# Row sums of 16384 x 1024 floats on one core: a two-row column tail, a first load of 4 rows, and the second group's load held until those are summed

## Chip, core, metric

One core of one Trainium2 chip. The metric is the device time of one execution in microseconds (us). The profile's span (first to last instruction) is 1.7 to 1.8 us shorter than the time of the same execution.

## The reference

```python
batch, seq, dim = 32, 512, 1024
x = np.random.randn(batch, seq, dim).astype(np.float32)     # 67.1 MB
def reference(x):
    return np.sum(x, axis=-1).astype(np.float32)            # 16384 sums
```

One addition for every four bytes read: the work is reading x once.

## The kernel before

Every partition gets 128 rows, in eight groups of 16. A group is one load of 8.39 MB (64 KB for each partition) into one of three buffers. VectorE sums the groups; in the last two groups ScalarE takes part of the rows, and the last row comes in three column pieces so that little is left to sum after the last byte.

```python
    nbig = J // BIG - 1                 # 7 groups of BIG = 16 rows, then a tail
    tail = [(8, 4), (4, 2), (2, 1)]     # rows, and how many of them ScalarE sums
    ...
        def act(dst, src, n):
            nc.scalar.activation(out=scratch[:, :n], in_=src,
                                 func=mybir.ActivationFunctionType.Copy, accum_out=dst)
    ...
        for i in range(nbig):
            t = inpool.tile([P, BIG * dim + 2], fp32)
            rows_of(t, 0, BIG, i * BIG, BIG // 2 if i == nbig - 1 else 0)
            if i % 3 == 2:
                store(nc.gpsimd, i - 2, i + 1)
        store(nc.gpsimd, nbig - 1, nbig)
    ...                                 # 8, 4, 2 rows, then one row for ScalarE
        cuts = [0, 384, 768, dim]       # the last row, in three column pieces
        for c0, c1 in zip(cuts, cuts[1:]):
            nc.sync.dma_start(out=last[:, c0:c1], in_=rows_from(j, 1)[:, 0, c0:c1])
        for i, (c0, c1) in enumerate(zip(cuts, cuts[1:])):
            if c1 < dim:
                vec(last[:, dim + i : dim + i + 1], last[:, c0:c1])
            else:                       # the third piece with the two partial sums
                vec(sums[:, j : j + 1], last[:, c0 : dim + i])
        store(nc.sync, nbig, nbig + 1)
```

(`...` marks what is left out.) The first load is moved ahead of the start-up barrier, to the very beginning of the program; loads 2 and 3 are issued right after the barrier.

## Time and profile before

| | before |
|---|---|
| time, median of 3 (range) | 162.79 us (162.73 to 162.85) |
| the profiled execution: time, span | 163.31 us, 161.5 us |
| hardware DMA queue, share of 16 engines' span | 97.1% |
| VectorE busy | 75% |
| 16-row sums start apart | 19.35 us, so 8.39 MB / 19.35 us = 433.5 GB/s |

The page of the profile of before. A queue's line gives packets, MB and the time of its packets as a share of sixteen DMA engines' span; a group's line gives busy time and mean ns, then the idle time before it and what ended it.

```profile
span 161.5 us, 124 instructions
...
DVE 121.4 (75%) x13; ACT 19.7 (12%) x33; POOL 2.4 (1%) x7
...
q1 hardware_dynamic: 2160, 67.12, 97.1%
q0 software_dynamic: 96, 0.06, 0.1%
...
L66 DVE TENSOR_REDUCE sums<-t 128x16 f32<-128x16384 f32 (+5 forms) x11 | 120.4, 10941 | 37.1 <-DMA t<-in_x_dram 37.0
```

Loads bound the kernel: their queue is busy nearly throughout, and all of VectorE's idle time ends with a load. The timeline of before, its start and its end (start and duration in us; the bracket is the idle time before and what ended it):

```profile
22.41 17.22 DVE L66 TENSOR_REDUCE sums<-t 128x16 f32<-128x16384 f32 x1 [22.41 <-DMA t<-in_x_dram]
41.74 17.22 DVE L66 TENSOR_REDUCE sums<-t 128x16 f32<-128x16384 f32 x1 [2.12 <-DMA t<-in_x_dram]
...
78.62 0.87 POOL L88 DMA_DIRECT2D out_dram<-sums  x1 [78.18 <-DVE sums L66]
...
138.55 8.69 DVE L66 TENSOR_REDUCE sums<-t 128x8 f32<-128x8192 f32 x1 [2.15 <-DMA t<-in_x_dram]
...
157.09 1.06 ACT L71 ACTIVATE scratch<-t 128x1024 f32<-128x1024 f32 x1
157.64 1.01 DVE L66 TENSOR_REDUCE t<-t 128x1 f32<-128x384 f32 x2 [0.68 <-DMA t<-in_x_dram]
158.06 0.19 ACT L71 ACTIVATION_READ_ACCUMULATOR scratch<-t 128x1 f32 x1
158.68 0.42 DVE L66 TENSOR_REDUCE sums<-t 128x1 f32<-128x258 f32 x1
159.17 0.35 SPq L88 DMA_DIRECT2D out_dram<-sums  x1
```

The first group can be summed at 22.41 us, and the stream alone needs 19.35 us for it. The last load packet ends at 157.90 us and its landing is signalled at 158.37; VectorE is then still on the piece before, so the last sum, 0.42 us, starts at 158.68, and a store follows. More quantities come from the trace's records of single DMA packets. A 64 KB packet takes 2.418 us in the steady stream; the sixteen first ones took 3.57 us on average, 1.15 us more. That is called the **start loss** below: the time that packets which start in the first 10 us take over the usual time of their size, per engine. The usual time is 2.418 us for 64 KB, 1.815 for 48 KB, 1.213 for 32 KB and 0.611 for 16 KB, the medians.

### The profile page before, as it was taken

Reading aid. Unit: us, or ns where it says so; the run is one execution under the profiler, and the core shown is the slowest. Engines: PE = TensorE matmul, PEld = TensorE weight load, DVE = VectorE, ACT = ScalarE, POOL = GpSimd, SP = SyncE. Lnnn points to the kernel's source line nnn. Section 1 sums busy time; section 2 is a strip of 40 time slices with the busy share of each in tenths; the row PEclk is TensorE's granted clock in tenths of the full one; section 3 lists DMA queues with packets and bytes.
Section 4 is the critical chain, followed back from the end, with each engine's and each line's share of the span. In section 5 each row is a group of like instructions: output and inputs, shape, how many; then the busy total and the mean of one; then the engine's idle time right before and its main releaser. Section 6 shows DMA issues by size and latency. Waiting matters only on the chain.

```text
span 161.5 us, 124 instructions
## 1 busy us (share of the span) xinstructions
DVE 121.4 (75%) x13; ACT 19.7 (12%) x33; POOL 2.4 (1%) x7
## 2 busy tenths in 40 slices
DVE  0000049998699968999499994999949997697883
ACT  3000000000000000000000000000000000698891
POOL 0000000000000000000200000000000001001000
DMA  8997998997997997996996996996997996999990
GB/s 260 519 438 341 519 406 373 519 438 341 519 454 325 519 471 308 519 487 292 519 493 293 519 487 292 519 487 292 519 454 325 519 487 292 391 491 389 410 392 14
DMA packets 2256, 67.18 MB, mean 416 GB/s; under 512 B 416, under 2 KB 848, under 8 KB 976
## 3 DMA queue, kind: packets, MB, share of 16 engines
q1 hardware_dynamic: 2160, 67.12, 97.1%
q0 software_dynamic: 96, 0.06, 0.1%
HBM read 67.11 MB, written 0.07 MB: 416 GB/s over the span
## 4 chain that ended last, share of the span: by engine, by line
DMA 74%; DVE 22%; SPq 1%; issue 0%; DVEq 0%
DMA t<-in_x_dram 74%; DVE sums L66 22%; SPq L81 1%; DVE t L66 1%; DVEq L66 0%
## 5 line engine op out<-in xcount | busy, mean ns | idle before, releaser
L66 DVE TENSOR_REDUCE sums<-t 128x16 f32<-128x16384 f32 (+5 forms) x11 | 120.4, 10941 | 37.1 <-DMA t<-in_x_dram 37.0
L71 ACT ACTIVATE scratch<-t 128x1024 f32<-128x1024 f32 x16 | 16.9, 1057 | 137.8 <-DMA t<-in_x_dram 137.3
L88 POOL DMA_DIRECT2D out_dram<-sums x3 | 2.2, 732 | 146.2 <-DVE sums L66 135.4
L71 ACT ACTIVATION_READ_ACCUMULATOR scratch<-t 128x1 f32 x16 | 3.0, 186 | 0.0
L66 DVE TENSOR_REDUCE t<-t 128x1 f32<-128x384 f32 x2 | 1.0, 549 | 0.7 <-DMA t<-in_x_dram 0.7
L71 ACT ACT_TABLE_LOAD x1 | 1.3, 1283 | 0.8 <-PEq L135 0.8
L135 POOL MEMSET const-float32-0.0<- 128x1 f32 x1 | 0.1, 98 | 0.2 <-issue 0.2
L135 POOL MEMSET const-bfloat16-1.0<- 128x1 bf16 x1 | 0.1, 101 | 0.0
L135 POOL MEMSET const-uint8-127<- 128x1 uint8 x1 | 0.1, 99 | 0.0
L135 POOL MEMSET const-float32-1.0<- 128x1 f32 x1 | 0.1, 98 | 0.0
## 6 DMA issues: line engine op xcount, KB each, us to landing
t<-in_x_dram SPq DMA_DIRECT2D x1, 4096.0 KB, 31.2
t<-in_x_dram SPq DMA_DIRECT2D x1, 2048.0 KB, 35.9
t<-in_x_dram SPq DMA_DIRECT2D x1, 1024.0 KB, 37.8
t<-in_x_dram SPq DMA_DIRECT2D x1, 512.0 KB, 38.6
t<-in_x_dram SPq DMA_DIRECT2D x2, 192.0 KB, 38.6
t<-in_x_dram SPq DMA_DIRECT2D x1, 128.0 KB, 38.4
t<-in_x_dram SPq DMA_DIRECT2D x7, 40.8
out_dram<-sums POOLq DMA_DIRECT2D x2, 24.0 KB, 7.9
```

The lines of the kernel that those rows point to most:

```text
L66: nc.vector.tensor_reduce(out=dst, in_=src, axis=mybir.AxisListType.X, op=mybir.AluOpType.add)
L71: nc.scalar.activation(out=scratch[:, :n], in_=src, func=mybir.ActivationFunctionType.Copy, accum_out=dst,)
L81: nc.sync.dma_start(out=block, in_=rows_from(j, n))
L88: eng.dma_start(out=out_v[:, g0:g1], in_=sums[:, g0 * BIG : g1 * BIG].rearrange("p (g j) -> p g j", j=BIG),)
L135: nc = _bacc.Bacc("TRN2", target_bir_lowering=False, num_devices=1)
```

## The change

Its intent: let the stream start without descriptors of later loads in its way (4 rows first, the second group held until VectorE has summed them); put all but the last 16 sums of each partition into one store that ScalarE issues near the end, in place of three GpSimd stores; share the two last rows between VectorE and ScalarE in three column pieces (640, 256, 128); and let ScalarE's unread results go to PSUM. The diff also adds `tc.manual_schedule()`. The core of the diff (comments added):

```diff
-        tc.tile_pool(name="scratch", bufs=1) as spool,
+        tc.tile_pool(name="unread", bufs=4, space=bass.MemoryType.PSUM) as upool,
+        tc.manual_schedule(),
...
-        for i in range(nbig):
-            t = inpool.tile([P, BIG * dim + 2], fp32)
-            rows_of(t, 0, BIG, i * BIG, BIG // 2 if i == nbig - 1 else 0)
-            if i % 3 == 2:
-                store(nc.gpsimd, i - 2, i + 1)
-        store(nc.gpsimd, nbig - 1, nbig)
+        for g in range(last):
+            t = inpool.tile([P, BIG * dim + 4], fp32)
+            if g == 0:
+                rows(t, 0, FIRST, 0, 0)                      # FIRST = 4
+                first = sums_of[-1]
+                rows(t, FIRST, BIG - FIRST, FIRST, 0)
+                continue
+            load = rows(t, 0, BIG, g * BIG, BIG // 2 if g == last - 1 else 0)
+            if g == 1:
+                tc.add_manual_dep(load.ins, first.ins.name, ...)
...
+        for width in pieces:                                 # 640, 256, 128
+            if len(parts) == k:
+                at += k                                      # room for partial sums
+            part = t[:, at : at + 2 * width].rearrange("p (n d) -> p n d", n=2)
+            nc.sync.dma_start(out=part, in_=rows_from(j, 2)[:, :, c : c + width])
...
+        w = t[:, at - 2 * width - k : at + k]
+        for i, part in enumerate(parts[:k]):
+            vec(w[:, i : i + 1], part[:, 0, :])
+            act(w[:, k + 2 * width + i : k + 2 * width + i + 1], part[:, 1, :], pieces[i])
+        store(nc.scalar, 0, last)
+        vec(sums[:, j : j + 2], w.rearrange("p (n d) -> p n d", n=2))
+        store(nc.sync, last, last + 1)
```

More of the change, by code (lines that the diff above doesn't have):

```diff
@@ L51, in rows_from @@
         return x_g[j // BIG, :, j % BIG : j % BIG + n, :]
-    nbig = J // BIG - 1
-    tail = [(8, 4), (4, 2), (2, 1)]
+    last = J // BIG - 1
+    FIRST = 4
+    pieces = (640, 256, 128)
     with (
         tc.tile_pool(name="in", bufs=3) as inpool,
-        tc.tile_pool(name="scratch", bufs=1) as spool,
+        tc.tile_pool(name="unread", bufs=4, space=bass.MemoryType.PSUM) as upool,
         tc.tile_pool(name="stage", bufs=1) as stpool,
+        tc.manual_schedule(),
     ):
         sums = stpool.tile([P, J], fp32)
-        scratch = spool.tile([P, dim], fp32)
         def vec(dst, src):
-            nc.vector.tensor_reduce(
+            return nc.vector.tensor_reduce(
                 out=dst, in_=src, axis=mybir.AxisListType.X, op=mybir.AluOpType.add
@@ L70, in act @@
         def act(dst, src, n):
+            unread = upool.tile([P, dim], fp32)
             nc.scalar.activation(
-                out=scratch[:, :n],
+                out=unread[:, :n],
                 in_=src,
@@ L76, in act, with rows @@
             )
-        def rows_of(t, a, n, j, n_act):
+        sums_of = []
+        def rows(t, a, n, j, n_act):
             nv = n - n_act
             block = t[:, a * dim : (a + n) * dim].rearrange("p (n d) -> p n d", d=dim)
-            nc.sync.dma_start(out=block, in_=rows_from(j, n))
-            if nv:
-                vec(sums[:, j : j + nv], block[:, :nv, :])
+            load = nc.sync.dma_start(out=block, in_=rows_from(j, n))
+            sums_of.append(vec(sums[:, j : j + nv], block[:, :nv, :]))
             for q in range(nv, n):
                 act(sums[:, j + q : j + q + 1], block[:, q, :], dim)
+            return load
         def store(eng, g0, g1):
@@ L91, in store @@
             )
-        for i in range(nbig):
-            t = inpool.tile([P, BIG * dim + 2], fp32)
-            rows_of(t, 0, BIG, i * BIG, BIG // 2 if i == nbig - 1 else 0)
-            if i % 3 == 2:
-                store(nc.gpsimd, i - 2, i + 1)
-        store(nc.gpsimd, nbig - 1, nbig)
-        t = inpool.tile([P, BIG * dim + 2], fp32)
+        for g in range(last):
[7 more added lines that the diff above has]
+            if g == 1:
+                tc.add_manual_dep(
+                    load.ins,
+                    first.ins.name,
+                    mybir.DependencyInfo(mybir.DependencyClass.Sync, mybir.DependencyReason.DATA),
+                    reason="no descriptors of later loads while the first ones start",
+                )
@@ L102 @@
+        t = inpool.tile([P, BIG * dim + 4], fp32)
         a = 0
-        for n, n_act in tail:
-            rows_of(t, a, n, nbig * BIG + a, n_act)
+        j = last * BIG
+        for n in (8, 4, 2):
+            rows(t, a, n, j + a, n // 2)
             a += n
-        rows_of(t, a, 1, nbig * BIG + a, 1)
-        a += 1
-        j = nbig * BIG + a
-        last = t[:, a * dim :]
-        cuts = [0, 384, 768, dim]
-        for c0, c1 in zip(cuts, cuts[1:]):
-            nc.sync.dma_start(out=last[:, c0:c1], in_=rows_from(j, 1)[:, 0, c0:c1])
@@ L115 @@
-        for i, (c0, c1) in enumerate(zip(cuts, cuts[1:])):
-            if c1 < dim:
-                vec(last[:, dim + i : dim + i + 1], last[:, c0:c1])
-            else:
-                vec(sums[:, j : j + 1], last[:, c0 : dim + i])
-        store(nc.sync, nbig, nbig + 1)
+        j += a
+        at = a * dim
+        k = len(pieces) - 1
+        parts = []
+        c = 0
+        for width in pieces:
[3 more added lines that the diff above has]
+            nc.sync.dma_start(out=part, in_=rows_from(j, 2)[:, :, c : c + width])
+            parts.append(part)
+            at += 2 * width
+            c += width
```

## The prediction

> **What bounds the kernel now.** The DMA stream. The page shows hardware-queue packets taking 97.1% of sixteen engines' span at a mean of 416 GB/s; VectorE is 75% busy and its idle 37.1 us is all put down to waits for loads. In the timeline the 16-row sums start 19.35 us apart: 8.39 MB / 19.35 us = 433.5 GB/s. The Trainium skill, "DMA: Bandwidth & Descriptors", section Specifications, gives 435 GB/s as the fabric ceiling; the trace agrees. Eight groups at 19.35 us are 154.8 us of the 161.5 us span, so everything else together is 6.7 us. In the DMA packets' records it divides so: 1.0 us before the first packet; a first packet per engine of 3.57 us where later ones take 2.42 us (1.15 us lost); about 1 us of short packets and stores inside the stream; last load packet ends at 157.90 us; then landing signal 0.47, last sums to 159.11, store issued at 159.17 and landed at 160.59, closing to 161.54. The time is 162.79 us, 1.3 us over the span. 2% faster would be 159.5 us, about half of those 6.7 us: hardly possible.
>
> **What the change does, by step.**
> 1. Start: first load of 4 rows, group 1 held until VectorE has summed them. Landing near 7 us, sum 4.4 us (as 128x4096 now), so the held load is issued near 11.5 us, while the 12-row load runs to about 22 us: no gap in the stream. Upper bound of the gain: the 1.15 us. But only one of the two issues that follow the first load is removed (the 12-row one is still issued at 0.8 us). And where seven loads are issued in a row (117 to 120.4 us) the packets under way take only 0.06 us longer, so descriptors alone look cheap. I count 0.4 us.
> 2. Three GpSimd stores in mid-stream go (packets of 0.18 us per engine). In their place ScalarE stores seven groups, 896 pieces of 64 B, 56 an engine; at the last store's 11 ns a packet, 0.6 us per engine, at the end. The skill, same page, section "Issuing engines are not separate DMA queues", says all issuers share the same 16 engines; so it competes with the last pieces or the last store. I count +0.3 us net, up to +0.9 if issuing 896 pieces is slow.
> 3. Tail: pieces of 640, 256 and 128 columns for two rows. Fixed part plus slope from the 384- and 258-column sums: VectorE needs 0.82 + 0.42 us, ScalarE 0.86 + 0.52 us (from its 1024-column 1.06 + 0.19). ScalarE ends near 0.7 us after the last load packet; the last sum, again 260 columns, 0.42 us, ends near 1.2 us after it, as now (1.20). No gain, no loss.
> 4. ScalarE results into PSUM: off the critical path.
>
> **Sum.** 162.79 - 0.4 - 0.2 (stream) + 0.3 = 162.5; I lean to a larger start gain: predicted 162.3 us, 8 in 10 between 161.4 and 163.2. Faster by over 2%: 0.02; within 2%: 0.96; slower by over 2%: 0.02.
>
> **What would show it.** Start: mean of the first packets (per 16 KB) and the landing of the first 16 rows, now 22.4 us; it should be 0.2 to 1.0 us earlier. GpSimd has only its memsets. Last load packet near 157.3 us; last sum about 1.2 us after it. ScalarE's store lands within 0.5 us of the last store.
>
> **What would make it wrong.** The held load leaves a gap; the first-packet loss is wholly caused by later issues (then near 161.7) or not at all (then near 162.8); ScalarE's store of 896 pieces takes over 2 us to issue or land (then 163 to 164.5); the last sum waits for ScalarE longer than worked out.

## The result

162.81 us, median of 4 (162.75 to 163.04), against 162.82 us for before, median of 4 (162.73 to 163.11). The ratio is 0.9999, 95% interval 0.9981 to 1.0016. Ratios are the mean time of one kernel's runs over that of the other's runs of the same rounds, so not quite the ratio of the medians. The time is inside the predicted range and the class "within 2%" was right; the point, 162.3 us, was 0.5 us too low: no gain came.

The page of the profile of after, with the lines that answer to those above (q10 is ScalarE's DMA queue):

```profile
span 161.0 us, 125 instructions
...
DVE 121.7 (76%) x14; ACT 18.5 (12%) x35; POOL 0.2 (0%) x4
...
q1 hardware_dynamic: 2544, 67.12, 97.4%
q10 hardware_dynamic: 912, 0.06, 0.3%
...
L68 DVE TENSOR_REDUCE sums<-t 128x16 f32<-128x16384 f32 (+6 forms) x12 | 120.5, 10042 | 36.5 <-DMA t<-in_x_dram 36.3
```

And the timeline of after:

```profile
7.23 4.42 DVE L68 TENSOR_REDUCE sums<-t 128x4 f32<-128x4096 f32 x1 [7.23 <-DMA t<-in_x_dram]
21.75 12.95 DVE L68 TENSOR_REDUCE sums<-t 128x12 f32<-128x12288 f32 x1 [10.10 <-DMA t<-in_x_dram]
41.10 17.22 DVE L68 TENSOR_REDUCE sums<-t 128x16 f32<-128x16384 f32 x1 [6.40 <-DMA t<-in_x_dram]
...
138.06 8.69 DVE L68 TENSOR_REDUCE sums<-t 128x8 f32<-128x8192 f32 x1 [2.33 <-DMA t<-in_x_dram]
...
156.94 1.15 DVE L68 TENSOR_REDUCE t<-t 128x1 f32<-128x640 f32 x2 [0.54 <-DMA t<-in_x_dram]
157.00 0.71 ACT L74 ACTIVATE unread<-t 128x640 f32<-128x640 f32 x1 [0.61 <-DMA t<-in_x_dram]
157.64 0.19 ACT L74 ACTIVATION_READ_ACCUMULATOR unread<-t 128x1 f32 x1
157.74 0.37 ACT L74 ACTIVATE unread<-t 128x256 f32<-128x256 f32 x1
157.80 0.41 ACTq L93 DMA_DIRECT2D out_dram<-sums  x1
158.04 0.19 ACT L74 ACTIVATION_READ_ACCUMULATOR unread<-t 128x1 f32 x1
158.26 0.42 DVE L68 TENSOR_REDUCE sums<-t 128x2 f32<-128x260 f32 x1 [0.17 <-ACT unread L74]
158.71 0.36 SPq L93 DMA_DIRECT2D out_dram<-sums  x1
```

Read side by side, the two profiles tell a tempting story: the first 16 rows are in at 21.75 us instead of 22.41, the lead of 0.66 us lasts to the end, and the span is 0.5 us shorter. The times don't follow. The reason: the profiled execution of before took 163.31 us, more than any of its timed runs (162.73 to 163.11), while that of after took 162.75, its fastest. (In the later groups before ranged up to 163.55 us, so 163.31 is within its habits; but it is not its typical time.) The two traces compare a slow execution of one kernel with a quick one of the other. Whether that was all, or whether the lead was real and lost elsewhere, was the question for the experiments.

### The profile page after: what moved, and what is told of

Read it like the earlier page. It is cut to its first block, busy times and chain, and to the rows that moved or that the text cites. A ratio compares the mean times of both kernels' runs of the same rounds, so it can differ in the third digit from the quotient of the medians.

```text
span 161.0 us, 125 instructions
## 1 busy us (share of the span) xinstructions
DVE 121.7 (76%) x14; ACT 18.5 (12%) x35; POOL 0.2 (0%) x4
## 4 chain that ended last, share of the span: by engine, by line
DMA 72%; DVE 25%; SPq 1%; issue 0%; ACTq 0%; ACT 0%; DVEq 0%
DMA t<-in_x_dram 72%; DVE sums L68 24%; SPq L86 1%; DVE t L68 1%; ACTq L93 0%; ACT unread L74 0%; DVEq L68 0%
## 5 line engine op out<-in xcount | busy, mean ns | idle before, releaser
L68 DVE TENSOR_REDUCE sums<-t 128x16 f32<-128x16384 f32 (+6 forms) x12 | 120.5, 10042 | 36.5 <-DMA t<-in_x_dram 36.3
L74 ACT ACTIVATE unread<-t 128x1024 f32<-128x1024 f32 (+2 forms) x17 | 16.2, 955 | 138.9 <-DMA t<-in_x_dram 138.9
L74 ACT ACTIVATION_READ_ACCUMULATOR unread<-t 128x1 f32 x17 | 3.2, 186 | 0.0
L68 DVE TENSOR_REDUCE t<-t 128x1 f32<-128x640 f32 (+1 forms) x2 | 1.1, 614 | 0.5 <-DMA t<-in_x_dram 0.5
```

Source lines behind the costliest of these rows:

```text
L68: return nc.vector.tensor_reduce(out=dst, in_=src, axis=mybir.AxisListType.X, op=mybir.AluOpType.add)
L74: nc.scalar.activation(out=unread[:, :n], in_=src, func=mybir.ActivationFunctionType.Copy, accum_out=dst,)
```

## The experiments

Theory A: the start loss of before's first profile was an unlucky one; the split and the hold do little. Theory B: the start is really 0.5 us quicker and after gives it back elsewhere. Two narrower ones came up on the way. Theory C: the split brings the sixteen engines into step, and engines in step lose more on the way. Theory D: later issues slow a first packet of 64 KB, and the hold prevents it. Twelve kernels ran, in three groups; those of a group share a chip and the runs of before. All gave correct results. Groups: before_again, start_only, no_hold, hold_all (before: 163.01 us, median of 11); nosplit, after_again, first_1, one_store (before: 163.11, 11); dephase, in_step, dephase4, nosplit_nohold (before: 163.18, 11).

The losses in each profile, from the packet records (us for each engine). "Spread" is the standard deviation of the engines' packet boundaries in the steady stream, modulo one packet, at 48 to 55 us:

```
                 first load   start loss   spread   loss on the way
before           16 rows        1.16        0.19       0.22
before_again     16 rows        0.72        0.18       0.17
nosplit          16 rows        0.74        0.17       0.20
nosplit_nohold   16 rows        0.71        0.23       0.25
after             4 rows        0.60        0.10       0.49
after_again       4 rows        0.55        0.09       0.17
start_only        4 rows        0.57        0.09       0.75
no_hold           4 rows        0.62        0.10       0.90
hold_all          4 rows        0.59        0.10       0.82
one_store         4 rows        0.64        0.09       0.58
first_1           1 row         0.66        0.16       0.48
dephase           4 + extra     1.63        0.29       0.25
dephase4          4 + extra     1.40        0.28       0.26
in_step           4 + extra     1.90        0.08       0.33
```

A row is one execution, and not always a typical one of its kernel: the profiled executions of start_only (163.18 us), hold_all (163.08) and one_store (163.79) were the slowest of their runs, those of before_again, after, after_again and dephase4 the fastest. So a row tells what that execution lost, not what its kernel usually loses.

### before_again: the kernel before, once more

No edit.

> The kernel before, unchanged. Theory A (chance): the profiled execution of before (163.31 us, span 161.5) was one with a slow start; most executions of before start as quickly as after does, so this profile shows a span near 161.0 us and the first 16 rows landed near 21.8 to 22.0 us. Theory B (given back): the start of before is really about 0.6 us slower, and after loses as much elsewhere: this profile again shows a first-row landing near 22.4 us and a span near 161.5. Both: ratio to before 1.000 within 0.2%, which also shows the noise of the comparison.

Measured: ratio to before 1.0014 (0.9998 to 1.0029), median 163.10 us; this is the same program, so a difference of 0.14% is noise here. The profiled execution took 162.85 us with a span of 161.1. Its timeline, first sums:

```profile
21.89 17.22 DVE L66 TENSOR_REDUCE sums<-t 128x16 f32<-128x16384 f32 x1 [21.89 <-DMA t<-in_x_dram]
41.23 17.22 DVE L66 TENSOR_REDUCE sums<-t 128x16 f32<-128x16384 f32 x1 [2.12 <-DMA t<-in_x_dram]
```

21.89 us, not 22.41, as theory A had it: most of the lead in the first comparison belonged to that one execution. Against after's 21.75 us, 0.14 us are left. How often before starts with the larger loss stays unknown: this profile is of the fastest of five executions (median 163.10), and 6 of the 33 executions of before in the three groups took 163.31 us or more.

### start_only: before, with only the 4-row load and the hold

```diff
-            rows_of(t, 0, BIG, i * BIG, BIG // 2 if i == nbig - 1 else 0)
+            if i == 0:
+                rows_of(t, 0, 4, 0, 0); first = sums_of[-1]
+                rows_of(t, 4, BIG - 4, 4, 0)
+                continue
+            load = rows_of(t, 0, BIG, i * BIG, BIG // 2 if i == nbig - 1 else 0)
+            if i == 1:
+                tc.add_manual_dep(load.ins, first.ins.name, ...)
```

> Before, with only the first load of 4 rows and the held second group taken over. Theory A: same time as before, 162.8 us (ratio 0.999 to 1.001). Theory B: the start's gain is here without what gives it back, 162.2 to 162.4 us (ratio about 0.996).

Measured: 162.80 us, ratio 0.9990 (0.9976 to 1.0005). That is at the edge of A's band and above B's 162.2 to 162.4, so B is not supported: taken alone, the start does not bring 0.5 us. The start loss is 0.57 us. But the profile also shows something that no theory had foreseen, in the timeline of start_only:

```profile
21.71 12.95 DVE L66 TENSOR_REDUCE sums<-t 128x12 f32<-128x12288 f32 x1 [10.07 <-DMA t<-in_x_dram]
41.22 17.22 DVE L66 TENSOR_REDUCE sums<-t 128x16 f32<-128x16384 f32 x1 [6.55 <-DMA t<-in_x_dram]
60.75 17.22 DVE L66 TENSOR_REDUCE sums<-t 128x16 f32<-128x16384 f32 x1 [2.32 <-DMA t<-in_x_dram]
80.33 17.22 DVE L66 TENSOR_REDUCE sums<-t 128x16 f32<-128x16384 f32 x1 [2.36 <-DMA t<-in_x_dram]
```

The groups arrive 19.51, 19.53 and 19.58 us apart instead of 19.35. The stream ran slower for a while, with nothing of the kernel's that explains it there, and in this execution, the slowest of the six, lost more than the start had won.

### no_hold: after, without the hold

```diff
-            if g == 1:
-                tc.add_manual_dep(load.ins, first.ins.name, ...)
```

> After, without the hold (the first load still has 4 rows). Theory A: same time as after, ratio to before 1.000 within 0.15%. Theory B with the hold as the cause of the quicker start: about 0.5 us slower than after, 163.3 us (ratio 1.003), first 16 rows landed near 22.3 us.

Measured: 163.19 us, ratio 1.0008 (0.9992 to 1.0024); the first 16 rows landed at 21.71 us and the start loss was 0.62 us, as with the hold. The time looks like B's figure, but not for B's reason: nothing was lost at the start. In the timeline of no_hold the loss sits between 99 and 119 us, where one group took 19.81 us:

```profile
99.14 17.22 DVE L68 TENSOR_REDUCE sums<-t 128x16 f32<-128x16384 f32 x1 [2.14 <-DMA t<-in_x_dram]
118.95 17.22 DVE L68 TENSOR_REDUCE sums<-t 128x16 f32<-128x16384 f32 x1 [2.59 <-DMA t<-in_x_dram]
```

### hold_all: after, with the 12-row load held too

```diff
+        idle = stpool.tile([P, 2048], fp32)
+        timer = nc.vector.memset(idle, 0.0)
-                rows(t, FIRST, BIG - FIRST, FIRST, 0)
+                load = rows(t, FIRST, BIG - FIRST, FIRST, 0)
+                tc.add_manual_dep(load.ins, timer.ins.name, ...)
```

> After, with the 12-row load held as well, by a VectorE memset that ends about 3 us after the start, so that no load at all is issued while the first packets start. If later issues slow the first packets (author's reason): first 16 KB packets near 0.61 us instead of 1.16 us, first 16 rows landed near 21.2 us, time about 162.2 us. If the slow first packets are the stream's own warming up: still near 1.1 us, and the time stays at 162.8 us within 0.2.

The timeline of hold_all, the memset and the first sums:

```profile
1.28 1.76 DVE L99 MEMSET idle<- 128x2048 f32 x1 [1.28 <-PEq L166]
7.12 4.42 DVE L68 TENSOR_REDUCE sums<-t 128x4 f32<-128x4096 f32 x1 [4.07 <-DMA t<-in_x_dram]
21.65 12.95 DVE L68 TENSOR_REDUCE sums<-t 128x12 f32<-128x12288 f32 x1 [10.11 <-DMA t<-in_x_dram]
```

The memset ended at 3.04 us and the 12-row load was issued at 3.07 us, when every engine's first packet was over (the last one ended at 2.49 us). Still the first packets took 1.17 us, against 1.16 in after, and the start loss was 0.59 us. The time was 162.64 us, ratio 0.9986 (0.9971 to 1.0001). So the first packets are slow with no later issue in the way: the reason that the change gives for its hold does not hold. This part of the start loss comes with starting, and what it consists of these runs don't show. The profile of hold_all had its own slow stretch (one group took 19.85 us, 118.40 to 138.25).

### nosplit: after, with a 16-row first load and a timed hold

```diff
+        idle = stpool.tile([P, 2048], fp32)
+        for _ in range(3):
+            first = nc.vector.memset(idle, 0.0)
-            if g == 0:
-                rows(t, 0, FIRST, 0, 0)
-                first = sums_of[-1]
-                rows(t, FIRST, BIG - FIRST, FIRST, 0)
-                continue
```

> After, with the first group loaded in one piece of 16 rows as in before; the second group's load is held by three VectorE memsets (about 6.5 us). Theory A (the size of the loss at the start is chance plus a fixed part, neither issues nor split matter): first packets lose 0.6 to 1.2 us an engine, as in the two profiles of before (0.72 and 1.16). Theory D (later issues do slow a 64 KB first packet): with the hold it is 0.6 us. Theory C (the split brings the engines into step and the stream then loses more on its way): the loss after 10 us is again 0.2 to 0.3 us an engine, as in the two profiles of before, not 0.5 to 0.9 as in the four with a split. Time 162.7 to 163.1 us by each.

Measured: 162.79 us (162.63 to 162.81), ratio 0.9982 (0.9969 to 0.9994). Start loss 0.74 us, first 16 rows at 21.93 us; against D, which wanted 0.6. Loss on the way 0.20 us, as C expected. The first sum in the timeline of nosplit:

```profile
21.93 17.22 DVE L68 TENSOR_REDUCE sums<-t 128x16 f32<-128x16384 f32 x1 [14.37 <-DMA t<-in_x_dram]
```

### nosplit_nohold: after, without split and hold

```diff
-            if g == 0:
-                rows(t, 0, FIRST, 0, 0)
-                first = sums_of[-1]
-                rows(t, FIRST, BIG - FIRST, FIRST, 0)
-                continue
-            if g == 1:
-                tc.add_manual_dep(load.ins, first.ins.name, ...)
```

> After, without the split and without the hold: of the change only the tail, the stores and PSUM are left. Theory D (later issues slow a first packet of 64 KB): start loss 0.7 to 1.2 us, varying, and a time 0.2 to 0.3 us over that of nosplit, near 163.0 us. Theory A: start loss 0.7 to 0.75 us in most executions and a time as nosplit, ratio to before 0.997 to 0.9995.

Measured: 162.87 us (162.81 to 163.06), ratio 0.9984 (0.9969 to 0.9998). Start loss 0.71 us with the later loads issued at once, 0.74 us with them held: theory D falls. The first sum in the timeline of nosplit_nohold:

```profile
22.02 17.22 DVE L68 TENSOR_REDUCE sums<-t 128x16 f32<-128x16384 f32 x1 [22.02 <-DMA t<-in_x_dram]
```

What is left of the change here, tail, stores and PSUM, already gives a ratio of 0.9984; the full change gave 0.9985 and 0.9999. Split and hold together add nothing that these runs can show.

### after_again: the kernel after, once more

No edit.

> The kernel after, unchanged, for a second profile and more times. Theory A: start loss 0.6 us, loss after 10 us anywhere between 0.2 and 0.9 us, ratio to before 0.998 to 1.001. Theory C: loss after 10 us over 0.45 us again.

Measured: 162.71 us, but from 162.46 to 163.41, ratio 0.9985 (0.9967 to 1.0004). Start loss 0.55 us. The profiled execution, 162.46 us, lost only 0.17 us on the way (0.32 counted from 10 us to the last load, as the expectation does). C's "over 0.45 again" was a miss: the same program lost 0.49 us in one execution and 0.17 in another.

### first_1: after, with a first load of 1 row

```diff
-    FIRST = 4
+    FIRST = 1
```

> After, with a first load of 1 row instead of 4. Theory A: start loss 0.6 us as with 4 rows, time as after within 0.2%. Theory C: engines at least as much in step, loss after 10 us over 0.45 us. If the loss at the start scaled with the first packet, it would be under 0.3 us and the first 16 rows would land near 21.4 us.

Measured: 163.17 us, ratio 1.0007 (0.9993 to 1.0022), a miss for A's "as after within 0.2%" when set against after_again of the same group (0.23% slower by the means, 163.19 against 162.82). The start loss, 0.66 us, is not smaller with a 4 KB first packet, as A had it; the first 16 rows landed at 22.21 us. The loss on the way was 0.48 us at a spread of 0.16 us.

### one_store: after, with all sums in the last store

```diff
-        store(nc.scalar, 0, last)
-        store(nc.sync, last, last + 1)
+        store(nc.sync, 0, last + 1)
```

> After, without ScalarE's store; the last store takes all eight groups, 1024 pieces of 64 B. Nothing hides them now: the last store lands about 0.6 us later after its issue (2.0 us instead of 1.43), if my estimate of 11 ns a piece and 56 pieces an engine holds, and the time is about 0.5 to 0.6 us longer than after. If the pieces cost nothing even exposed, 1.4 us and no longer time.

Measured: 163.37 us, ratio 1.0022 (1.0009 to 1.0035); by the means of the group 163.42 against 162.82 for after_again, 0.6 us longer. From issue to landing the last store took 2.18 us instead of 1.43. The lists of DMA issues (queue, count, KB, us from issue to landing), of after first, then of one_store:

```profile
out_dram<-sums ACTq DMA_DIRECT2D x1, 56.0 KB, 2.1
out_dram<-sums SPq DMA_DIRECT2D x1, 8.0 KB, 1.4
```

```profile
out_dram<-sums SPq DMA_DIRECT2D x1, 64.0 KB, 2.2
```

So the prediction's cost for 896 small pieces was sound, 0.75 us instead of the estimated 0.6, but in after it is hidden: ScalarE issues at 157.80 us, before it has finished its own last sum, and its store landed at 159.92 us, 0.23 us before the last one. The Trainium skill, "DMA: Bandwidth & Descriptors", section "Issuing engines are not separate DMA queues", says that all issuers run on the same engines; what after gains is not bandwidth but the time between the last loads and the last store, in which the engines were idle.

### in_step, dephase, dephase4: the engines' step, set on purpose

All three are after with 12 KB a partition loaded a second time into an unread tile, between the first two loads; the number of partitions sets how many engines get a packet. n is 16 in in_step, 8 in dephase and 4 in dephase4.

```diff
+                again = stpool.tile([n, 3 * dim], fp32)
+                nc.sync.dma_start(
+                    out=again.rearrange("p (n d) -> p n d", d=dim), in_=x_g[0, :n, 0:3, :])
                 rows(t, FIRST, BIG - FIRST, FIRST, 0)
```

> The control of dephase: the same 12 KB, but by sixteen partitions, one extra packet on every engine, so they stay in step (spread 0.1 us). Both theories: about 0.45 us longer than after. Theory C: loss after 9 us over 0.45 us. Theory A: anywhere from 0.2 to 0.95.

> After, with 12 KB loaded once more by eight partitions between the first two loads, into a tile that nobody reads: eight DMA engines get one extra packet of about 0.46 us, the others none, so the engines run further out of step (spread of their packet ends 0.2 to 0.3 us instead of 0.1). Theory C (engines in step lose more on the way): loss after 9 us 0.2 to 0.3 us an engine instead of 0.3 to 0.95, and the time 0.2 to 0.4 us shorter than that of in_step. Theory A (mid-stream losses are chance): anywhere from 0.2 to 0.95, no difference of time from in_step beyond noise.

> As dephase, with the extra packet on four engines only: spread about 0.2 us. Theory C: loss after 9 us 0.2 to 0.35 us and a time like that of dephase. Theory A: anywhere from 0.2 to 0.95.

Measured: in_step 164.59 us (ratio 1.0087, 1.0070 to 1.0104), dephase 164.31 us (1.0068, 1.0051 to 1.0084), dephase4 164.25 us (1.0067, 1.0053 to 1.0081). The spreads came out as meant: 0.08, 0.29 and 0.28 us. The time difference between in_step and dephase, 0.3 us, is what C had predicted, and still C is not confirmed: the packet records place the difference before 10 us (1.90 against 1.63 us), not on the way (0.33 against 0.25, with 0.10 of the 0.33 right behind the extra load). None of the three had a slow stretch: after 10 us their 64 KB packets took 2.421 or 2.422 us in the median and none over 2.431, while every other profile has 9 to 97 packets over 2.468. What they lost on the way is mostly these 3 to 4 ns a packet. So in_step, whose engines ran closest in step of all, had no slow stretch, and dephase had none to be spared. By the expectation's own measure, after 9 us, in_step lost 0.51 us and dephase 0.43, but 0.18 of each lie in the last pieces, after 150 us. C as stated has fallen: being in step is not enough.

All three cost far more than expected: 1.1 to 1.4 us over before, where some 0.45 us over after had been worked out from the rate. In in_step the extra packets took 0.46 us on the first engines and 1.07 on the last, and the 48 KB packets behind them 2.6 to 3.2 us instead of 1.82. The first two sums of in_step show it:

```profile
7.80 4.42 DVE L68 TENSOR_REDUCE sums<-t 128x4 f32<-128x4096 f32 x1 [7.80 <-DMA t<-in_x_dram]
23.71 12.95 DVE L68 TENSOR_REDUCE sums<-t 128x12 f32<-128x12288 f32 x1 [11.49 <-DMA t<-in_x_dram]
```

The 12 rows come 15.9 us behind the 4 rows instead of 14.5. The Trainium skill, "SBUF — State Buffer", section "Door 1: The DMA port swizzle", says that a transfer's bandwidth depends on how many of 16 ports its partitions reach; by the formula given there, the first sixteen partitions reach four, the first eight two and the first four one, so that each of the three loads puts four partitions on every port that it reaches. That fits the extra packets of in_step and dephase, which did take longer one after another (up to 1.07 us), but not those of dephase4 (0.46 to 0.61 us). And in dephase4 the first 48 KB packets of all sixteen engines took 2.60 to 3.03 us, though twelve of the engines had no extra packet. So the ports alone don't account for the delay; its cause stays open.

## Why the prediction was right, and where it was off

**The class and the range** were right, for the reason given: the stream takes 154.8 us of the span and the change doesn't touch it, so all terms together could not reach 2%.

**The sum** predicted 162.79 - 0.4 - 0.2 + 0.3 and then leaned to 162.3. Its terms, beside what the profiles showed:

| term | predicted | measured | how |
|---|---|---|---|
| start | -0.4 (at most -1.15) | -0.14 | landing of the first 16 rows 21.89 us (before_again) against 21.75 (after); start loss 0.72 on average in three profiles with 16 rows first (0.71 to 0.74, without the first one of before), 0.60 in six with 4 rows (0.55 to 0.64) |
| stream, GpSimd's stores gone | -0.2 | -0.01 | their packets go, 0.18 us with 0.03 us of completion packets in it, but the short pieces cost 0.17 us more (all load packets at the usual time of their size: 155.17 us against 155.34) |
| ScalarE's store | +0.3 | +0.01 | last store 1.42 us from issue to landing before, 1.43 after |
| last sum after the last load packet | 0 | 0 | 1.20 us before, 1.21 after |
| from the last landing to the span's end | not named | -0.14 | 0.95 us before, 0.81 after; start_only and nosplit both have 0.88, so no one part of the change brings it alone |
| loss on the way | not named | 0 to +0.7 | 0.17 to 0.25 us in four profiles with 16 rows first; 0.17 to 0.90 in the six of the table with 4 rows first |

The gains that the profiles show, 0.14, 0.01 and 0.14 us less 0.01, make 0.3 us. The times keep 0 to 0.25 of it (ratios 0.9999 and 0.9985).

**Step 1 is the one that failed, in its size.** "Upper bound of the gain: the 1.15 us ... I count 0.4 us" was built on the start loss of one execution. That execution, at 163.31 us, lay above every timed run: an execution slower than all timings should not have been the measure of what can be saved. The prediction's "The time is 162.79 us, 1.3 us over the span" shows the mix: the execution with that span took 163.31 us, 1.8 us over it. before_again lost 0.72 us at the start, and in place of 0.4 us the landing of the first 16 rows came 0.14 us earlier. The warning inside the step was right: descriptors are cheap (the packets under way were slowed by only 0.06 us when seven loads were issued in a row), and hold_all showed that the remaining 0.6 us stay when nothing else is issued. The prediction's own clause "not at all (then near 162.8)" is what came.

**Step 2** was right about the cost of 896 small pieces (0.75 us when exposed, in one_store) and wrong about its place: ScalarE's store is issued early enough to be hidden. It was also wrong on the stream term, for it counted the GpSimd packets that go and not the short packets that come: pieces of 2560, 1024 and 512 bytes take 102, 46 and 27 ns, where the rate of the 64 KB packets would give 94, 38 and 19.

**Step 3**, no gain and no loss in the tail, held: 1.21 us against "near 1.2". ScalarE ended 0.75 us after the last load packet (158.23 against 157.48), predicted "near 0.7".

**Step 4** held: ScalarE's 1024-column sum took 1010 ns into PSUM and 1057 into SBUF, off the critical path. The Trainium skill, "ScalarE: Activation LUTs", section "Step-by-step: what each stage is for", says that PSUM is the quicker destination; the trace agrees, by 47 ns, though the result tiles also went from one to four and no run separates the two.

**Where the 0.3 us went.** In the profile of after, slower stretches in mid-stream took most of them (0.49 us lost on the way against 0.22 in before). In six of the eight profiles with a split first load and engines in step or nearly so, the stream lost 0.48 to 0.90 us on the way; in all six with 16 rows first or with engines set apart it lost 0.17 to 0.26. That is an association found after the fact. The direct test did not bear it out (in_step lost 0.33, without a slow stretch), after_again lost 0.17, three of the six were the slowest execution of their kernel, and the groups ran on different chips. The times don't settle it either: in the three groups the executions of a kernel with a split first load and no extra one spread over 0.47 to 0.95 us, those of nosplit and nosplit_nohold over 0.18 and 0.25, but those of before, which has no split, over 0.67 to 0.76. It stays open whether the split causes the slow stretches. It also stays open why executions of before vary more (162.78 to 163.52 us beside nosplit_nohold's 162.81 to 163.06): the two profiles of before differ by 0.44 us in their start loss, and that part of nosplit_nohold is the same as in before.

No version clearly beats both kernels: nosplit (0.9982), nosplit_nohold (0.9984) and hold_all (0.9986) are ahead of before by 0.2 to 0.3 us, and none is ahead of after_again (0.9985); before_again, the same program as before, gave 1.0014.

## What to carry to other kernels

Before taking an excess in one profile as what a change can save, compare that execution's time with the timed runs, and profile the unchanged kernel twice; here the second profile took away most of the expected gain. When a kernel is at the rate of its stream, cost what a change adds to the stream (short pieces) as carefully as what it removes (stores). The store that cost 0.75 us at the end in one_store was hidden in after, where another engine issued it while the last sums were still running.

## What the Trainium skill lacked or had wrong

- "DMA: Bandwidth & Descriptors" gives a first-byte latency for loads from SP of about 0.6 us and does not say from when. Here the first packet starts 1.00 us after the issue starts and 0.63 us after it ends (0.38 us of issue).
- No page has the start loss: the first packets of a stream take 0.55 to 0.74 us an engine more than later ones of their size (once 1.16), whether their load is 1, 4 or 16 rows and whether or not other loads are issued behind it.
- "DMA: Bandwidth & Descriptors", section "Measured", has 425 GB/s for 16 MB (issued from GpSimd); the steady stream here runs at 433.5 GB/s, nearer to the page's ceiling of 435.
- "SBUF — State Buffer" has the ports, but no page says, outside remote DMA, that a small load to few partitions can delay the large load queued behind it: 192 KB to sixteen partitions, 0.45 us an engine at the stream's rate, cost the stream about 1.3 us an engine of start loss besides (1.90 against 0.60), and 48 KB to four partitions about 0.8 (1.40 against 0.60).
- No page warns that a steady stream can slow by 0.2 to 0.5 us for a group (19.51 to 19.85 us instead of 19.35) without a cause in the kernel.
